# A long depthwise convolution accumulated in a PSUM bank, with GpSimd making the low parts of the weights

## The chip, the cores and the metric

The kernel runs on one core of one Trainium2 chip. The metric is the time of one execution on the device in microseconds (us), lower is better. The core has five engines that each work through an instruction list of their own in order: TensorE (PE in the profile, PEld for its weight loads), VectorE (DVE), ScalarE (ACT), GpSimd (POOL) and the DMA queue of SyncE (SP). They wait for one another by semaphores. SBUF holds the operands; PSUM has 8 banks of 128 x 512 float32, into which TensorE writes its products.

## The reference, cut to what matters

512 tokens of width 1024 go through two transformer blocks in float32. The second block, where the change lies, is one long set of products of the same normalised input with a wide projection, in eight parts of 1024 features, and what is made of them:

```python
g    = (h @ W3 + b3) * sigmoid(h @ W4 + b4)   # gated input
c    = dwconv(g, b_conv)                      # causal, depthwise, 31 taps:
                                              # c[f, t] = conv_b[f] + sum_j w[f, j] * g[f, t - 30 + j]
c    = silu(group_norm(c) * ...)              # group = 128 features
v    = layer_norm(gelu(h @ Wv + bv))          # mixed over the tokens by ws
u    = gelu(h @ W0 + b0)
za   = silu(h @ W2 + b2) * u * (mix(v) + ...)
m1   = sigmoid(h @ W6 + b6) * (za @ w_pa)     # and so on: z_b, m2, output projection
```

## The kernel before

**Layout.** Activations are feature-major: a tile `a` is 128 features by 512 tokens, and 1024 features are eight tiles, counted by `m`. A weight comes in pieces of 128 x 1024 (tile `wr`) by DMA. Each float32 product is done as three passes in a rounded format: every operand is split into a high and a low part. For a weight piece ScalarE casts the high part (`wh<-wr`, a CAST) and a second engine subtracts it to get the low part (`wl<-wr,wh`, a TENSOR_TENSOR). So a piece costs TensorE 8 k-tiles x 3 passes = 24 matmuls, and it can't go through the second operand of any k-tile before its `wl` is there. There are three buffers each for `wr`, `wh` and `wl`.

**Who makes the low part.** `weight` counts the pieces; of every four, `SHARE[0]` go to GpSimd and the others to VectorE, from the start of the second block until the products `m1` are done, `SHARE[1]` after that. It is (3, 0) before: three of four on GpSimd in the stage.

**The stage.** `block2` runs these phases on TensorE, one after the other: the gated input (8 steps of two pieces each), v (two halves of the features, 4 pieces each), u (8 pieces), za (8 pieces, each with four small matmuls for the token mix), m1 (8 steps of two pieces each). VectorE evacuates what each step leaves in PSUM, and at the end of each step it gets some taps of the convolution from `taps(n)`: one tap is one `scalar_tensor_tensor` on 128 x up to 512 elements, accumulator = gated input * weight + accumulator, 31 of them one after the other for each `m`, the first a `tensor_scalar` that adds the bias. `TAPS` says how many taps each phase's steps get. What of a convolution is finished goes through `group_norm`: split (a ScalarE cast waits for the last tap), two matmuls against a centring matrix, a square, a sum, a reciprocal root (`pow` on GpSimd, the tiles `s`).

**The order.** The kernel's code is traced once, and a scheduler in the framework puts the instructions of each engine in a fixed order by its own model of costs; taps of two convolutions may so alternate on VectorE. At run time no engine reorders anything. All instructions are recorded in one helper, so that the profile gives line L95 for nearly everything; the tiles' names tell them apart. In the stage `wl` is the low part of a weight piece, `a<-a,vecs,a` on VectorE a tap, and `a<-ps,vecs,a` 128x512 an evacuation from PSUM.

Of the kernel before, what the change touches and what calls it, by code (L numbers as in the profile page):

```python
# [27 lines left out]
# columns of the per-feature vectors, one array [128, NV]  # L28
# [9 lines left out]
_FIRST = 8  # columns that the first product needs  # L38

TAPS = (4, 3, 6, 6, 11)  # taps of the long convolution per step of each phase of the second block  # L40
# units of the attention after which the other projections follow
FILL = (0, 2, 8, 10, 4, 6, 12, 14, 14, 15, 17, 20, 23, 26, 30)
BANKS = {"score": (0, 1, 2, 3), "turn": (4, 5), "out": (6,), None: (7,)}  # PSUM banks by use
A_AT = (0, 2)  # steps of the values' projection after which a unit of the attention starts
SHARE = (3, 0)  # of four weight pieces, how many GpSimd splits: during the convolution, after it
RAW = 2  # m-tiles of the second block that are scaled after the product
# [7 lines left out]
class _Slot:  # L54
    """A slot of a pool, returned to it when its last view is dropped."""
# [8 lines left out]
class V:  # L64
    """A view of a tile that keeps its slot."""
# [38 lines left out]
class _Slots:  # L104
    """Slots of one pool, given out in program order, the one longest free first."""
# [15 lines left out]
class Body:  # L121
    """Activations are kept feature-major: features on partitions, the 512 tokens on the free axis.

    A float32 product is carried by three float32r passes: each operand is split exactly into a
    high and a low part, and high*high + high*low + low*high is accumulated in PSUM.
    """
# [36 lines left out]
    def weight(self, src, raw=None):  # L163
        """One [128, <=1024] piece of a weight: loaded and split."""
        nc = self.nc
        n = src.shape[-1]
        raw = raw or self.load(src)
        hi = self.whi.tile([P, 1024], F32R)
        lo = self.wlo.tile([P, 1024], F32R)
        nc.scalar.copy(hi[:, :n], raw[:, :n])  # L170
        self.pieces += 1
        eng = nc.gpsimd if self.pieces % 4 < self.share else nc.vector
        eng.tensor_tensor(lo[:, :n], raw[:, :n], hi[:, :n].bitcast(F32), op=ALU.subtract)
        return hi, lo

    def split(self, x, gain=None, out=None):
        """x (times a per-partition gain) in two exact parts."""
        nc = self.nc
        shape = list(x.shape)
        hi, lo = out if out else (self.a(shape, F32R), self.a(shape, F32R))  # L180
        if gain is None:
            nc.scalar.copy(hi, x)
            nc.vector.tensor_sub(lo, x, hi.bitcast(F32))
        else:
            nc.scalar.activation(hi, x, AF.Identity, bias=0.0, scale=gain)
            nc.vector.scalar_tensor_tensor(lo, x, gain, hi.bitcast(F32), op0=ALU.mult, op1=ALU.subtract)
        return hi, lo

    def mm(self, ps, l, r, start, stop):
        """l, r: pairs (hi, lo) of APs."""  # L190
        nc = self.nc
        nc.tensor.matmul(ps, l[0], r[0], start=start, stop=False)
        nc.tensor.matmul(ps, l[0], r[1], start=False, stop=False)
        nc.tensor.matmul(ps, l[1], r[0], start=False, stop=stop)

    def dense(self, src, rhs, n=S, raw=None):
        """One m-tile of W^T x: src = list of (weight piece, its k-tiles)."""
        ps = self.ps((P, n))
        k, last = 0, len(rhs) - 1
        for piece in src:  # L200
            w = self.weight(piece, raw)
            raw = None
            for kk in range(piece.shape[-1] // P):
                s = slice(kk * P, (kk + 1) * P)
                self.mm(ps, (w[0][:, s], w[1][:, s]), rhs[k], k == 0, k == last)
                k += 1
        return ps

    def square_sum(self, x, acc, last=False, scale=1.0):
        """Adds the squares of x to the list acc: one running sum and the last square apart."""  # L210
        nc = self.nc
        sq = self.a(x.shape)
        nc.scalar.activation(sq, x, AF.Square, scale=scale)
        if last or not acc:
            acc.append(sq)
        else:
            nc.gpsimd.tensor_tensor(acc[0], acc[0], sq, op=ALU.add)

    def token_sum(self, acc, n):
        """Sums over the partitions, token-major: [128, n]."""  # L220
        ps = self.ps((P, n))
        for j, t in enumerate(acc):
            for i in range(n):
                self.nc.tensor.matmul(ps[:, i:i + 1], t[:, i * P:(i + 1) * P], self.ones[:, 0:1],
                                      start=(i == 0 and j == 0), stop=(i == n - 1 and j == len(acc) - 1))
        acc.clear()
        return ps
# [9 lines left out]
    def bcast(self, r, n):  # L237
        """A token-major column per token tile, over all partitions: PSUM [128, n*128]."""
        ps = self.ps((P, n * P))
        for i in range(n):  # L240
            self.nc.tensor.transpose(ps[:, i * P:(i + 1) * P], r[:, i:i + 1].to_broadcast([P, P]), self.ident)
        return ps
# [46 lines left out]
    def nsa(self):  # L289
# [13 lines left out]
        # the first product goes on as x comes in  # L303
# [11 lines left out]
        def shifted(p):  # L315
            """Two m-tiles of a compression input: [(token parity, 64), token] of each group."""
# [13 lines left out]
        def token_gates():  # L330
            """Rows 0:48 from the weights' high parts, 64:112 from the low ones; turned and added."""
# [14 lines left out]
        def hidden(key, c2, between):  # L346
            """gelu(blocks W1), transposed: PSUM [hidden half, 2, (group, block)]."""
# [41 lines left out]
        def cmp_values(c2, between):  # L389
            """Per group [(head, block), head, (high, low)], zero outside of a head's own rows."""  # L390
# [25 lines left out]
        def values(q):  # L416
            """Values of the two dense branches, token-major: [t, group, (high, low)]."""
# [56 lines left out]
        def compressed_a(g):  # L474
            """Compressed branch of one group: probabilities, [t, t tile, head, block]."""
# [25 lines left out]
        def compressed_b(s):  # L501
            """Transposed and split: [(head, block), t]."""
# [5 lines left out]
        def dense_a(h, b):  # L508
            """Exponentials of one dense branch of one head, t tile by t tile, and their sums."""
# [4 lines left out]
            for tiles in ((0, 1), (2,), (3,)):  # L514
# [6 lines left out]
                # the blocks on the diagonal; those of the first two tiles lie side by side  # L521
# [18 lines left out]
        def dense_b(es):  # L540
            """Transposed and split: (parts, first column, columns, first token) per key tile."""
# [20 lines left out]
        # probabilities of the last two key tiles, of two units in turn; their first block stays zero  # L562
# [8 lines left out]
        def dense_c(h, b, parts, pc):  # L571
            """Product with the values; all three branches of a head in one bank."""
# [24 lines left out]
        # projections of the compression's inputs, statistics of x meanwhile  # L597
# [127 lines left out]
    def residual(self, src, rhs, x, gain, scale=None):  # L725
        """x + rhs W, m-tile by m-tile; its split parts times the gain; its squares' sum."""
# [95 lines left out]
    def conv(self, acc, src, taps, first, last, width, eng):  # L822
        """Taps first..last-1 of a causal depthwise convolution; tap width-1 is the current token."""
# [35 lines left out]
    def block2(self, x3, xs, acc, acc2, gain):  # L859
# [32 lines left out]
        hc, cacc, yb = [], [], []  # L892
# [3 lines left out]
        def taps(n):  # L896
            """The next taps of the convolution."""
            nonlocal done
            end = min(len(work), done + n)
            while done < end and work[done][0] < len(hc):  # L900
                m, j = work[done]
                w = self.vec("b_conv", 31 * m + 30 - j)
                if j == 0:
                    cacc[m] = self.a()
                    nc.vector.tensor_scalar(cacc[m], hc[m], w, self.vec("conv_b", m), op0=ALU.mult, op1=ALU.add)
                else:
                    acc = cacc[m][:, j:S]
                    nc.vector.scalar_tensor_tensor(acc, hc[m][:, 0:S - j], w, acc, op0=ALU.mult, op1=ALU.add)
                done += 1
                if j == 30:  # L910
                    hc[m] = None

        def group_norm(m):
            """Normalised over the group's channels and times the gain; in steps."""
# [27 lines left out]
        # gated input of the convolution  # L942
        self.share = SHARE[0]
        for m in range(KD):
# [20 lines left out]
            taps(TAPS[0])  # L965
        # v, token-major: gelu, layer norm, spatial mix
# [36 lines left out]
        # the layer norm's shift passes the mix as shift * (sum of a row of ws); bs added  # L1003
# [87 lines left out]
        # per-layer embedding  # L1091
# [18 lines left out]
        # the last projection by halves of the tokens: one half is normalised and stored under the other  # L1110
# [83 lines left out]
def _mt(w):  # L1194
    """[K, N] -> [N/128, 128 (k), K/128 * 128 (n)]"""
# [4 lines left out]
def _tok(w):  # L1200
    """[K, N] -> [N/512, K/256, 128 (k), 2 * 512 (n)]"""
# [73 lines left out]
```

## Time and profile before

| | |
|---|---|
| timed runs | 1505.55, 1504.51, 1504.46 us; median 1504.51 us |
| profiled execution | span 1505.2 us (no other time is listed for it) |
| PE busy | 1437.1 us, 95% |
| DVE busy | 977.6 us, 65% |
| ACT busy | 654.7 us, 43% |
| POOL busy | 403.4 us, 27% |
| instructions | 18564 |

TensorE is busy in 95% of the span, so a kernel of the same products can at best lose what TensorE idles, and what it spends at a lower clock. The page's strips of 40 slices show both in one place: PE falls from 9 tenths to 7 or 8 in the slices from 900 to 1240 us, which is the stage above, and DVE reads 9 there for four slices in a row, which it does nowhere else. The views of the next section but one are taken from there.

### The profile page before, as it was taken

The page shows a single profiled execution, that of the slowest core. Times are in us where ns is not written, and L with a number is a line of the kernel's source. Part 1 is how long each engine was busy: PE and PEld are TensorE (multiplying, and loading weights), DVE is VectorE, ACT ScalarE, POOL GpSimd, SP SyncE. Part 2 cuts the span into 40 slices and gives each one's busy share as a digit, 9 for nine tenths or more (in the row PEclk, how much of TensorE's full clock was granted, in tenths as well). Part 3 has the DMA queues.
Part 4 walks back from the last instruction along what each step waited for, and adds up shares of the span by engine and source line. Part 5 has one row for each costly group of instructions (what it writes and reads, how often), then busy time and mean ns, then how long its engine had stood idle before and what let it go on. Part 6 is the DMA issues. An engine that isn't in the chain of part 4 may idle for free. (4 is left out here: it accounts for less than half of the span.)

```text
span 1505.2 us, 18564 instructions
## 1 busy us (share of the span) xinstructions
PE 1437.1 (95%) x7106; PEld 1197.1 (80%) x7106; DVE 977.6 (65%) x1431; ACT 654.7 (43%) x1127; POOL 403.4 (27%) x333
## 2 busy tenths in 40 slices
PE   7999999999999999999999998897998899999997
PEld 6787778888888888888888887675886778888897
DVE  4868898885455465555533359999769953444564
ACT  4857778774344333323233333112233354432362
POOL 4022446451211311111111242333343441011213
PEclk9999999999999999999999999998999999999998
DMA  5241112114222333333333342221321222333331
GB/s 201 84 126 57 43 30 70 57 57 151 79 76 87 98 97 94 95 96 97 95 101 91 108 123 70 83 72 56 98 82 59 76 79 84 112 98 99 98 98 57
DMA packets 41385, 133.00 MB, mean 88 GB/s; under 512 B 5200, under 2 KB 7504, under 8 KB 41296
## 3 DMA queue, kind: packets, MB, share of 16 engines
q1 hardware_dynamic: 39568, 129.71, 28.5%
q10 hardware_dynamic: 1728, 2.10, 0.4%
q8 instruction: 56, 0.92, 0.2%
q14 instruction: 33, 0.27, 0.1%
HBM read 129.70 MB, written 2.10 MB: 88 GB/s over the span
## 5 line engine op out<-in xcount | busy, mean ns | idle before, releaser
L95 PE MATMUL ps<-a,wh 128*128 128x512 f32 (+1 forms) x3136 | 966.0, 390 | 9.4 <-ACT a L95 4.2
L95 PEld LDWEIGHTS ps<-a,wh 128*128 128x128 f32 x3136 | 588.3, 190 | 128.5 <-ACT a L95 5.4
L95 PE MATMUL ps<-a,wl 128*128 128x512 f32 (+1 forms) x1560 | 608.7, 390 | 22.6 <-DVE wl L95 14.9
L95 ACT CAST wh<-wr 128x1024 fp32r<-128x1024 f32 (+1 forms) x225 | 234.5, 1044 | 534.2 <-PE ps L95 351.5
L95 PEld LDWEIGHTS ps<-a,wl 128*128 128x128 f32 x1560 | 296.4, 190 | 84.9 <-DVE wl L95 17.4
L95 DVE TENSOR_TENSOR a<-ps,a 128x512 f32<-128x512 f32 (+5 forms) x284 | 169.8, 614 | 264.4 <-PE ps L95 210.3
L95 DVE TENSOR_TENSOR wl<-wr,wh 128x1024 fp32r<-128x1024 f32 x183 | 238.1, 1302 | 129.4 <-ACT wh L95 128.0
L95 POOL TENSOR_TENSOR a<-a,a 128x512 f32<-128x512 f32 (+1 forms) x106 | 138.9, 1314 | 597.8 <-ACT a L95 482.3
L95 DVE SCALAR_TENSOR_TENSOR a<-a,vecs,a 128x511 f32<-128x511 f32 (+25 forms) x332 | 288.3, 906 | 8.7 <-ACT a L95 6.3
L95 PE MATMUL ps<-a,a 128*128 128x256 f32 (+4 forms) x1180 | 209.2, 322 | 8.3 <-ACT a L95 8.3
L95 PEld LDWEIGHTS ps<-a,a 128*128 128x128 f32 x1180 | 165.3, 192 | 20.7 <-ACT a L95 10.6
L95 POOL TENSOR_TENSOR wl<-wr,wh 128x1024 fp32r<-128x1024 f32 x42 | 116.0, 2763 | 184.8 <-ACT wh L95 179.9
L95 POOL TENSOR_TENSOR a<-a,s 128x512 f32<-128x512 f32 (+3 forms) x140 | 115.3, 852 | 184.4 <-DVE s L95 106.6
L95 DVE TENSOR_TENSOR a<-a,a 128x512 fp32r<-128x512 f32 (+3 forms) x172 | 118.9, 697 | 23.7 <-ACT a L95 15.6
L95 ACT CAST a<-a 128x512 fp32r<-128x512 f32 (+1 forms) x124 | 76.4, 622 | 97.3 <-DVE a L95 78.6
L95 ACT ACTIVATE a<-a 128x512 f32<-128x512 f32 (+1 forms) x114 | 61.5, 551 | 117.9 <-DVE a L95 117.8
L95 PE MATMUL ps<-wh,a 128*128 128x512 f32 (+1 forms) x320 | 95.4, 379 | 6.7 <-ACT wh L95 6.7
L95 ACT ACTIVATE a<-ps,s 128x256 f32<-128x256 f32 (+4 forms) x148 | 77.5, 529 | 27.3 <-DVE s L95 23.7
L95 ACT CAST a<-ps 128x384 fp32r<-128x384 f32 (+2 forms) x132 | 62.9, 488 | 32.7 <-PE ps L95 27.5
L95 PEld LDWEIGHTS ps<-wh,a 128*128 128x128 f32 x320 | 59.8, 195 | 17.4 <-ACT wh L95 7.5
L95 DVE TENSOR_REDUCE s<-ps 128x1 f32<-128x128 f32 (+4 forms) x136 | 62.1, 491 | 5.1 <-PE ps L95 4.3
L95 PE MATMUL ps<-wl,a 128*128 128x512 f32 (+1 forms) x160 | 60.6, 379 | 4.3 <-DVE wl L95 2.7
(78 smaller groups left out, 611.6 us busy)
## 6 DMA issues: line engine op xcount, KB each, us to landing
wr<-in_w_in_dram SPq DMA_DIRECT2D x56, 512.0 KB, 3.6
wr<-in_ffn_gate_dram SPq DMA_DIRECT2D x22, 512.0 KB, 3.6
wr<-in_ffn_val_dram SPq DMA_DIRECT2D x22, 512.0 KB, 3.5
wr<-in_ffn_d_dram SPq DMA_DIRECT2D x16, 512.0 KB, 3.5
wr<-in_nsa_w_in_dram SPq DMA_DIRECT2D x15, 512.0 KB, 3.6
wr<-in_ca_wk_dram SPq DMA_DIRECT2D x8, 512.0 KB, 3.6
wr<-in_ca_wv_dram SPq DMA_DIRECT2D x8, 512.0 KB, 3.5
wr<-in_nsa_w_out_dram SPq DMA_DIRECT2D x8, 512.0 KB, 3.6
```

What stands on the lines that cost most here:

```text
L95: return lambda *a, **k: f(*[_raw(x) for x in a], **{n: _raw(x) for n, x in k.items()})
```

## The change

The accumulator of a convolution is a tile of PSUM instead of SBUF, and one copy by ScalarE (`to_sbuf`) brings it to SBUF after the last tap. GpSimd makes all low parts of the stage. The taps per step change from 4, 3, 6, 6, 11 (gated input, v, u, za, m1) to 4, 5, 5, 4, 10, with 7 in place of 4 from the third step of the gated input on. Comments are left out as well, which changes no instruction.

```diff
-TAPS = (4, 3, 6, 6, 11)  # taps of the long convolution per step of each phase of the second block
+TAPS = (4, 5, 5, 4, 10, 7)
...
-SHARE = (3, 0)  # of four weight pieces, how many GpSimd splits: during the convolution, after it
+SHARE = (4, 0)
...
-        hc, cacc, yb = [], [], []
+        hc, cacc, yb, run = [], [], [], [None]
...
                 if j == 0:
-                    cacc[m] = self.a()
-                    nc.vector.tensor_scalar(cacc[m], hc[m], w, self.vec("conv_b", m), op0=ALU.mult, op1=ALU.add)
+                    run[0] = self.ps()
+                    nc.vector.tensor_scalar(run[0], hc[m], w, self.vec("conv_b", m), op0=ALU.mult, op1=ALU.add)
                 else:
-                    acc = cacc[m][:, j:S]
+                    acc = run[0][:, j:S]
                     nc.vector.scalar_tensor_tensor(acc, hc[m][:, 0:S - j], w, acc, op0=ALU.mult, op1=ALU.add)
                 done += 1
                 if j == 30:
                     hc[m] = None
+                    cacc[m] = self.to_sbuf(run[0])
+                    run[0] = None
...
-            taps(TAPS[0])
+            taps(TAPS[0] if m < 2 else TAPS[5])
```

VectorE has 1400 instructions instead of 1414 and ScalarE 980 instead of 972. The first place is VectorE's list in the gated input, around the evacuation of the fourth to fifth step. In the kernel before, `a_8192` and `a_8688` are the accumulators of the first two convolutions (in SBUF), `a_8189` and `a_8262` their inputs, `wl_8514` is the low part of a weight piece, and `a_8472<-ps_8440` the evacuation:

```order
L95 SCALAR_TENSOR_TENSOR a_8192<-a_8189,vecs,a_8192 128x498
L95 TENSOR_TENSOR wl_8514<-wr_8511,wh_8513 128x1024
L95 SCALAR_TENSOR_TENSOR a_8192<-a_8189,vecs,a_8192 128x497
L95 SCALAR_TENSOR_TENSOR a_8688<-a_8262,vecs,a_8688 128x500
L95 SCALAR_TENSOR_TENSOR a_8192<-a_8189,vecs,a_8192 128x496
L95 SCALAR_TENSOR_TENSOR a_8688<-a_8262,vecs,a_8688 128x499
L95 SCALAR_TENSOR_TENSOR a_8192<-a_8189,vecs,a_8192 128x495
L95 SCALAR_TENSOR_TENSOR a_8472<-ps_8440,vecs,a_8471 128x512
```

With the change the same place reads as follows; `ps_8192` and `ps_8558` are the accumulators, now in PSUM, and `a_8478<-ps_8446` is the evacuation of that step:

```order
L95 SCALAR_TENSOR_TENSOR ps_8192<-a_8189,vecs,ps_8192 128x498
L95 SCALAR_TENSOR_TENSOR ps_8558<-a_8262,vecs,ps_8558 128x500
L95 SCALAR_TENSOR_TENSOR ps_8192<-a_8189,vecs,ps_8192 128x497
L95 SCALAR_TENSOR_TENSOR ps_8558<-a_8262,vecs,ps_8558 128x499
L95 SCALAR_TENSOR_TENSOR ps_8192<-a_8189,vecs,ps_8192 128x496
L95 SCALAR_TENSOR_TENSOR a_8478<-ps_8446,vecs,a_8477 128x512
L95 SCALAR_TENSOR_TENSOR ps_8192<-a_8189,vecs,ps_8192 128x495
L95 SCALAR_TENSOR_TENSOR ps_8558<-a_8262,vecs,ps_8558 128x498
```

The weight's low part has left VectorE's list; the taps of two convolutions alternate as before, and 13 to 15 of them stand between two evacuations of this phase, against 13 to 17 and a `wl` in every second step before.

The second place is ScalarE's list at the start of the phase m1. Before, `a_9774` is the gate of the first step, `a_10357<-a_9842` the cast at the start of a group norm (it waits for a last tap, `a_9842` being that accumulator), and `wh_9898` the high part of the first piece of `w_pa`:

```order
L95 CAST wh_9866<-wr_9864 128x1024
L95 ACT_TABLE_LOAD
L95 ACTIVATE a_9774<-ps_9775,vecs 128x512
L95 CAST a_10357<-a_9842 128x512
L95 CAST wh_9898<-wr_9896 128x1024
```

With the change, `a_9795` is that gate, `a_10045<-ps_9741` the new copy of a finished accumulator, and `wh_9917` the first piece of `w_pa`:

```order
L95 CAST wh_9885<-wr_9883 128x1024
L95 ACT_TABLE_LOAD
L95 ACTIVATE a_9795<-ps_9796,vecs 128x512
L95 COPY a_10045<-ps_9741 128x512
L95 CAST wh_9917<-wr_9915 128x1024
```

The cast of a weight piece stands directly behind an instruction that waits for VectorE's last tap, as it did before; a second such place is new, at the start of za, where `a_9349<-ps_9113` stands ahead of the cast of the piece `wh_9396`.

The third place is GpSimd's list at the start of the gated input, where `s_8069` and `s_8081` are the two reciprocal roots of the normalisation that the stage starts with, and the `wl` are low parts; lines with a plus are new there, those with a minus are gone:

```order
 L95 TENSOR_TENSOR s_8069<-s_8067,neghalf 128x4
+L95 TENSOR_TENSOR wl_8232<-wr_8229,wh_8231 128x1024
 L95 TENSOR_TENSOR s_8081<-s_8079,neghalf 128x4
 L95 TENSOR_TENSOR wl_8273<-wr_8270,wh_8272 128x1024
 L95 TENSOR_TENSOR wl_8304<-wr_8301,wh_8303 128x1024
```

One low part that VectorE made has moved in between the two roots.

## Rows read from the trace of the kernel before

**Rows 1.** The page: the span, and the busy time of each engine with its share of the span and its number of instructions.

```profile
span 1505.2 us, 18564 instructions
PE 1437.1 (95%) x7106; PEld 1197.1 (80%) x7106; DVE 977.6 (65%) x1431; ACT 654.7 (43%) x1127; POOL 403.4 (27%) x333
```

**Rows 2.** The stage in windows (start:end, length; then for PE, PEld, DVE, ACT and POOL the busy us and the number of instructions; the granted TensorE clock, the busy share of the DMA engines, GB/s).

```profile
900.00:920.00 20.00, 15.20 (x58) 11.39 (x57) 19.31 (x27) 8.65 (x11) 3.57 (x2) 0.91 0.24 79
920.00:960.00 40.00, 40.00 (x178) 33.16 (x177) 40.00 (x42) 9.72 (x11) 16.33 (x6) 1.00 0.31 93
960.00:1060.00 100.00, 79.95 (x317) 63.01 (x316) 98.89 (x139) 20.02 (x24) 30.46 (x10) 0.90 0.20 63
1060.00:1120.00 60.00, 60.00 (x285) 50.36 (x284) 36.67 (x38) 20.72 (x26) 26.15 (x12) 1.00 0.33 95
1120.00:1180.00 60.00, 48.16 (x211) 38.27 (x210) 59.63 (x71) 19.23 (x26) 20.15 (x10) 0.94 0.20 63
1180.00:1240.00 60.00, 58.38 (x279) 48.00 (x278) 46.65 (x60) 30.71 (x37) 26.80 (x13) 1.00 0.27 80
```

**Rows 3.** The stretches of the stage in which TensorE was granted the lower of its two clock levels (0.50 or 0.51 of 2.4 GHz, that is 1.2 GHz), in windows with the same columns.

```profile
909.20:912.60 3.40, 3.04 (x7) 2.47 (x8) 3.40 (x7) 0.89 (x1) 0.00 (x0) 0.50 0.04 14
970.60:977.50 6.90, 3.14 (x8) 2.48 (x9) 6.76 (x12) 0.00 (x0) 0.00 (x0) 0.51 0.30 88
1018.40:1025.30 6.90, 4.44 (x10) 3.16 (x11) 6.90 (x6) 2.66 (x3) 5.11 (x2) 0.51 0.27 76
1052.50:1059.40 6.90, 5.61 (x13) 4.46 (x14) 6.83 (x12) 0.00 (x0) 1.23 (x1) 0.51 0.27 76
1137.90:1141.30 3.40, 2.99 (x7) 2.41 (x8) 3.32 (x6) 2.15 (x3) 0.77 (x1) 0.50 0.51 146
1172.00:1175.40 3.40, 3.40 (x9) 2.64 (x10) 3.40 (x6) 0.00 (x0) 0.00 (x0) 0.50 0.78 245
```

**Rows 4.** What TensorE waited for from 900 to 1240 us: engine, tile and line waited for, us in total, times, longest.

```profile
PE ps L95 <- DVE wl L95: 16.0, 5, 7.1
PE ps L95 <- POOL wl L95: 9.3, 5, 5.2
PE ps L95 <- ACT wh L95: 6.7, 3, 4.1
PE ps L95 <- ACT a L95: 4.2, 2, 3.3
PE ps L95 <- DVE a L95: 2.1, 3, 0.8
```

**Rows 5.** VectorE's costliest groups from 914 to 1224 us that the change touches (taps, low parts of weights, first taps), and GpSimd's low parts from 880 to 1240 us: line, engine, operation, out<-in, shape, number; busy us, mean ns of one; idle before and what ended it.

```profile
L95 DVE SCALAR_TENSOR_TENSOR a<-a,vecs,a 128x499 f32<-128x499 f32 (+22 forms) x240 | 213.9, 941 | 1.3
L95 DVE TENSOR_TENSOR wl<-wr,wh 128x1024 fp32r<-128x1024 f32 x11 | 15.3, 1392 | 0.5 <-ACT wh L95 0.5
L95 DVE TENSOR_SCALAR a<-a,vecs 128x512 f32<-128x512 f32 x8 | 8.4, 1058 | 0.0
...
L95 POOL TENSOR_TENSOR wl<-wr,wh 128x1024 fp32r<-128x1024 f32 x39 | 108.8, 2792 | 178.5 <-ACT wh L95 173.6 <-PE ps L95 4.9
```

**Rows 6.** VectorE beside GpSimd in the timeline (start, us, engine, operation, number), first around 963 us, then around 1481 us; in each the POOL row is what ran on GpSimd at the time.

```profile
962.63 0.72 DVE L95 SCALAR_TENSOR_TENSOR a<-a,vecs,a 128x491 f32<-128x491 f32 x1
963.27 0.74 DVE L95 SCALAR_TENSOR_TENSOR a<-ps,vecs,a 128x512 f32<-128x512 f32 x1
963.93 2.20 DVE L95 SCALAR_TENSOR_TENSOR a<-a,vecs,a 128x486 f32<-128x486 f32 x1
962.36 3.25 POOL L95 TENSOR_TENSOR wl<-wr,wh 128x1024 fp32r<-128x1024 f32 x1 [8.54 <-ACT wh L95]
...
1480.95 0.47 DVE L95 SCALAR_TENSOR_TENSOR a<-a,vecs,ps 128x256 f32<-128x256 f32 x1
1480.01 2.50 POOL L95 TENSOR_TENSOR a<-a,a 128x256 f32<-128x256 f32 x3 [0.85 <-ACT a L95]
```

**Rows 7.** The evacuations of two successive steps of the gated input on VectorE in the timeline; that at 963.27 us in the group above is the fourth of the same row of steps.

```profile
917.96 0.75 DVE L95 SCALAR_TENSOR_TENSOR a<-ps,vecs,a 128x512 f32<-128x512 f32 x1 [0.19 <-PE ps L95]
934.93 0.74 DVE L95 SCALAR_TENSOR_TENSOR a<-ps,vecs,a 128x512 f32<-128x512 f32 x1
```

**Rows 8.** Prices: a run of nine alternating taps and a run of four taps of one accumulator (timeline), one low part on GpSimd (timeline), an evacuation and a tap of nearly the same size, VectorE reading and writing PSUM, VectorE with its second input in PSUM on 256 elements, an instruction of VectorE on 128x4 elements, and ScalarE's copy of a PSUM bank (groups by shape: number, busy us, mean ns).

```profile
935.59 5.94 DVE L95 SCALAR_TENSOR_TENSOR a<-a,vecs,a 128x502 f32<-128x502 f32 x9
1065.60 3.05 DVE L95 SCALAR_TENSOR_TENSOR a<-a,vecs,a 128x497 f32<-128x497 f32 x4
1062.64 2.39 POOL L95 TENSOR_TENSOR wl<-wr,wh 128x1024 fp32r<-128x1024 f32 x1 [8.90 <-ACT wh L95]
L95 DVE SCALAR_TENSOR_TENSOR a<-ps,vecs,a 128x512 f32<-128x512 f32 x16 | 11.8, 744 | 14.8 <-PE ps L95 14.3 <-ACT a L95 0.5
L95 DVE SCALAR_TENSOR_TENSOR a<-a,vecs,a 128x510 f32<-128x510 f32 x8 | 5.9, 738 | 0.0
L95 DVE TENSOR_TENSOR ps<-ps,a 128x512 f32<-128x512 f32 x4 | 2.5, 683 | 0.0
L95 DVE SCALAR_TENSOR_TENSOR a<-a,vecs,ps 128x256 f32<-128x256 f32 x10 | 4.3, 474 | 2.2 <-ACT a L95 2.2
L95 DVE TENSOR_SCALAR s<-ps 128x4 f32<-128x4 f32 x3 | 0.4, 147 | 0.0
L95 ACT COPY a<-ps 128x512 f32<-128x512 f32 x2 | 1.1, 586 | 0.0
```

## The prediction, made before the result was known

> **What bounds the kernel now.** I read the page first: TensorE is busy for 1437.1 of 1505.2 us [rows 1], so all that a change outside of the products can save is its idle time and what it spends at the lower clock. The windows then say where that lies. From 900 to 1240 us TensorE idles 4.80 us (900 to 920), 20.05 us (960 to 1060), 11.84 us (1120 to 1180) and 1.62 us (1180 to 1240), 38.3 us together, and none from 920 to 960 and from 1060 to 1120 [rows 2]. [...] The same matmuls take half of that at the full clock, so the dips cost 22.62 / 2 = 11.3 us: 1.5 at the start, 6.6 from 960 to 1060, 3.2 after 1120. The stage has 38.3 + 11.3 = 49.6 us to give.
>
> What TensorE waits for is in the waits: 16.0 us for a low part that VectorE makes, 9.3 us for one that GpSimd makes, 6.7 us for a high part, 6.3 us for split activations [rows 4]. VectorE is the cause of more than the first. It is busy for 40.00 of 40, 98.89 of 100 and 59.63 of 60 us in the windows from 920 to 1060 and from 1120 to 1180 [rows 2], and it falls behind: its evacuations at 917.96 and 963.27 are three steps apart, 15.1 us for each [rows 6, 7], while TensorE needs 48 matmuls of 40.00 / 178 = 0.225 us, 10.8 us, for a step of two pieces [rows 2]. A low part in its list comes as late as VectorE is. The wait for a GpSimd piece is partly this too: the reciprocal root ahead of that piece in GpSimd's list waits for VectorE's statistics.
>
> And VectorE is so slow because it stands still. While GpSimd makes a low part (962.36, 3.25 us), an operation with one input in PSUM passes at its usual 0.74 us, while the tap after it, with two inputs in SBUF, takes 2.20 us instead of 0.72 [rows 6]. Near the end of the program the taps' other form, one input in SBUF and one in PSUM, takes 0.47 us while a GpSimd operation runs [rows 6], as in the mean of all ten of them, 474 ns [rows 8]. Over the stage the 240 taps after the first ones take 213.9 us, mean 941 ns [rows 5], against 735 ns or so for one left alone: four in a row take 3.05 us [rows 8]. That is 240 x 0.206 = 49 us of standing still or sharing.
>
> **The change part by part.**
>
> *Accumulator in PSUM.* A tap then has one SBUF input, the form that passed above. I take its own time as unchanged: 744 ns for an evacuation of 512 elements that reads PSUM, 738 ns for a tap of 510 from SBUF; a PSUM-to-PSUM operation takes 683 ns [rows 8]. The start-to-start distance is (5.94 - 0.73) / 8 = 0.65 us where two convolutions alternate and (3.05 - 0.73) / 3 = 0.77 us on one accumulator [rows 8]. That a chain through PSUM costs more no row shows. Below I put 0.77. Above I put 0.89: the 0.744 us of the PSUM reader and behind it the 0.147 us of a nearly empty instruction, as if the two did not overlap at all [rows 8]. I take 0.77 to 0.79, since the PSUM rows lie next to the SBUF ones. The gain of the part is 49 us of VectorE's time, not yet TensorE's.
>
> [...]
>
> *All low parts on GpSimd.* VectorE loses 11 of them from 914 to 1224 us, 15.3 us [rows 5], and three outside of that; more important, TensorE no longer waits for anything in VectorE's list except by a PSUM bank or an activation. GpSimd gets 14 x 2.39 = 33 us more [rows 5, 8], in a stage where it is busy for 3.57 + 16.33 + 30.46 + 26.15 + 20.15 + 26.80 = 123 us of 340 [rows 2]: about half. That a list of GpSimd pieces feeds TensorE is shown from 1060 to 1120 us: TensorE is busy for all 60.00 us [rows 2]. The piece between the two roots at the start delays the second by 2.4 us at most; it is hidden behind the first step's second product, by about 1 us, and would cost up to 1.4 us if that cover were missing.
>
> *New distribution.* In the gated input 13 to 15 taps lie between two evacuations (the order above): 16 operations at 0.65 us are 10.5 us against TensorE's 10.8. VectorE keeps pace where it took 15.1. In v 20 taps on one accumulator stand before the first half's evacuation: 15.4 us, against 4 x 24 x 0.225 = 21.6 us for the half's four pieces. Then the gap at 967 (7.1 us, the longest wait in rows 4), that at 1015 to 1022 and that of the reciprocal root lose their cause. I put 960 to 1060 at zero: 20.05 + 6.6 = 26.7 us saved.
>
> *Copies.* Eight of 0.586 us [rows 8] on an engine that is busy for a third of the stage [rows 2] cost nothing by themselves. But each waits for a last tap, and the casts of weights stand behind it. Two such places are near their limit: za's first piece and `w_pa`'s first piece. In za a step of VectorE is three evacuating operations of about 0.7 us and the 4 taps of 0.77, 5.2 us, plus up to 2 us for one of its two-SBUF operations that meets a low part, against 24 x 0.225 + 4 small matmuls, some 6.3 us for TensorE: a lag of up to 0.9 us a step, 4 to 7 us at the end of za. I count 1.5 us of waiting at the first place (0 to 4), 5 at the second (0 to 7), and the 3.2 us of clock that follow such a gap today. The 1.62 us from 1180 to 1240 stay. So 11.3 of 16.7 us are left after 1120; saved: 5.4 us.
>
> *PSUM.* One or two banks of eight are held by accumulators. v is where that is tight: its two halves take four each, and the fourth of the second half must wait for the first half's last evacuation. VectorE is at its place there with about a microsecond to spare; a miss costs 1 to 3 us.
>
> *Start.* The 4.80 and 1.5 us at 900 to 920 belong to the scaling and splitting of the activations, which nothing changes: kept.
>
> **Sum.** 49.6 us less 6.3 at the start and 11.3 after 1120 leave 32 us. 1505.2 - 32 = 1473.2 in the profiled execution's terms, whose span lies 0.7 us above the median of the timed runs (1504.5): **1472 us**.
>
> **The rivals.**
>
> *Partly given back (1486 to 1501 us).* The copies put ScalarE in VectorE's wake: where VectorE is 5 us late at each of four to six copies, TensorE waits as often, and each gap brings 3 us of lower clock, as 2.99 and 3.40 us of busy time at the lower clock behind the gaps after 1120 show [rows 3]. Four times 5 + 1.6 give back 26 us: 1498. For it: a cast that waits behind a group norm's split is the 6.7 us for high parts already [rows 4]. Against it: the first six copies have half a step or more of slack if VectorE keeps pace.
>
> *No gain (1501.5 to 1507.5).* If the taps still stood still beside GpSimd, the 14 more low parts would add blocks as fast as the 15.3 us leave. The 0.47 us beside a GpSimd operation speak against it [rows 6].
>
> *Slower.* One mechanism: a tap that reads and writes the same PSUM bank, 31 times in a chain, is slow. Before, VectorE spends (213.9 + 15.3 + 8.4) / 248 = 0.96 us for each tap [rows 5], and has 23.3 us idle from 1060 to 1120 to catch up in [rows 2]. So it decides from 0.96 + 23.3 / 248 = 1.05 us for each tap; at 1.15 us VectorE needs 25 us more than it has, and the time is about 1530. Against it stand the 683 ns of the operation within PSUM, which isn't chained, however [rows 8]. [...]
>
> *More than forecast (under 1460).* za keeps pace too, and only the start is left: 1504.5 - 43 = 1461; under that only if the start gained as well.
>
> **How the numbers follow.** I give the forecast, 1460 to 1486 us, 0.71; partly given back 0.14; no gain 0.04; slower 0.06; under 1460 us 0.05. The likeliest one's own range, from the bounds above: with both copies free 1504.5 - 43 = 1461; with a tap of 0.89, v and m1 lag by 3 us each, both copies cost their most (4 + 7 in place of 6.5) and one more dip of 3 us follows: 1472 + 6 + 4.5 + 3 = 1486. To hold 8 in 10 the range takes some of the partial case: 1460 to 1490. A measurement of this kernel tells about 0.2%, 3 us, from no change. Faster by more than that: 0.71 + 0.14 + 0.05 = 0.90; within it 0.04; slower 0.06.
>
> **What would show it.** Right: taps as `ps<-a,vecs,ps` with a mean of 0.70 to 0.75 us and none of 2 to 3 us; GpSimd's low parts at about 2.4 us, none of 4 to 8; no `wl` on VectorE before 1220 us; VectorE's evacuations in the gated input 10.8 us apart; TensorE idle for 10 to 14 us from 900 to 1240, its waits on `ACT wh` and the split activations, none on a VectorE `wl`; the lower clock near 909 and once or twice in the last third. Wrong: taps over 0.9 us (slower rival), long taps beside GpSimd (no gain), or a list of `ACT wh` waits behind the copies (partly given back).

## The result and the profile after

The changed kernel takes 1465.08 us (median of four runs, 1464.92 to 1465.96) against 1505.03 us for the kernel before, run beside it. The ratio is 0.9738 with a 95% interval of 0.9727 to 0.9750: 40 us faster, where 1472 us were forecast. The page of after, its span and busy times:

```profile
span 1463.2 us, 18587 instructions
PE 1424.6 (97%) x7106; PEld 1190.2 (81%) x7106; DVE 922.6 (63%) x1417; ACT 659.7 (45%) x1135; POOL 415.9 (28%) x347
```

The span is 42.0 us shorter than that of [rows 1], where the timed runs differ by 40. The windows of the stage, columns as in [rows 2], say where:

```profile
900.00:920.00 20.00, 15.19 (x58) 11.41 (x57) 18.64 (x27) 8.65 (x11) 6.18 (x3) 0.91 0.25 79
920.00:960.00 40.00, 40.00 (x178) 33.14 (x177) 37.15 (x58) 10.30 (x12) 17.82 (x8) 1.00 0.31 93
960.00:1060.00 100.00, 100.00 (x439) 82.09 (x438) 91.48 (x135) 30.09 (x37) 39.78 (x18) 1.00 0.31 90
1060.00:1120.00 60.00, 59.32 (x294) 49.84 (x293) 35.33 (x46) 22.76 (x32) 34.31 (x18) 1.00 0.28 82
1120.00:1180.00 60.00, 56.73 (x268) 46.08 (x267) 43.50 (x66) 30.39 (x38) 26.36 (x13) 1.00 0.29 86
1180.00:1240.00 60.00, 60.00 (x291) 49.99 (x290) 34.83 (x50) 32.93 (x40) 16.32 (x10) 1.00 0.30 85
```

From 960 to 1060 us TensorE is busy for all 100.00 us; it was 79.95. In the stage it idles 4.81 + 0.68 + 3.27 = 8.8 us in place of 38.3, so 29.5 us of idle time went. The granted clock is 1.00 in every window but the first, whose dip is the one of before. TensorE's busy total fell by 12.5 us (1437.1 to 1424.6) for the same 7106 matmuls. Most of that is the lower clock's: of the 11.3 us that the prediction counts for it in [rows 3], all but the 1.5 us at the start, 9.8 us, are gone. The other 2.7 us no view here assigns. 29.5 + 12.5 = 42.0, and TensorE's busy and idle time before and behind the stage is the same in both traces. What TensorE still waits for from 900 to 1240 us:

```profile
PE ps L95 <- ACT a L95: 4.1, 2, 3.3
PE ps L95 <- POOL wl L95: 2.4, 2, 1.8
PE ps L95 <- DVE a L95: 1.8, 3, 0.8
PE ps L95 <- ACT wh L95: 0.4, 1, 0.4
```

The 16.0 us for low parts of VectorE in [rows 4] are gone, those for GpSimd's went from 9.3 to 2.4. The groups that answer to [rows 5], VectorE from 914 to 1224 us and GpSimd's low parts from 880 to 1240 us:

```profile
L95 DVE SCALAR_TENSOR_TENSOR ps<-a,vecs,ps 128x483 f32<-128x483 f32 (+24 forms) x240 | 170.3, 735 | 4.5
L95 DVE TENSOR_SCALAR ps<-a,vecs 128x512 f32<-128x512 f32 x8 | 6.3, 804 | 12.7 <-ACT a L95 12.7
...
L95 POOL TENSOR_TENSOR wl<-wr,wh 128x1024 fp32r<-128x1024 f32 x53 | 126.9, 2395 | 170.3 <-ACT wh L95 161.5 <-PE ps L95 6.2 <-DVE a L95 2.6
```

The taps fell from 941 to 735 ns, and GpSimd's low parts from 2792 to 2395 ns, so a tap and a low part no longer stand still for each other. VectorE's evacuations of the gated input in the timeline:

```profile
928.62 0.75 DVE L95 SCALAR_TENSOR_TENSOR a<-ps,vecs,a 128x512 f32<-128x512 f32 x1 [1.31 <-PE ps L95]
939.50 0.75 DVE L95 SCALAR_TENSOR_TENSOR a<-ps,vecs,a 128x512 f32<-128x512 f32 x1 [0.43 <-PE ps L95]
950.38 0.75 DVE L95 SCALAR_TENSOR_TENSOR a<-ps,vecs,a 128x512 f32<-128x512 f32 x1 [0.55 <-PE ps L95]
```

They are 10.9 us apart, the pace of TensorE's steps, and each waits for TensorE; in [rows 6, 7] three steps took 15 us each. The engine that is late has changed sides.

### The profile page after: what moved, and what is told of

Same layout as the page of the kernel before. It is cut to its first block, busy times and chain, and to the rows that moved or that the text cites. A ratio compares the mean times of both kernels' runs of the same rounds, so it can differ in the third digit from the quotient of the medians.

```text
span 1463.2 us, 18587 instructions
## 1 busy us (share of the span) xinstructions
PE 1424.6 (97%) x7106; PEld 1190.2 (81%) x7106; DVE 922.6 (63%) x1417; ACT 659.7 (45%) x1135; POOL 415.9 (28%) x347
## 4 chain that ended last, share of the span: by engine, by line
PE 87%; DVE 7%; ACT 2%; issue 1%; POOL 1%; DMA 1%; POOLq 0%; SPq 0%; ACTq 0%
PE ps L95 87%; DVE a L95 5%; ACT a L95 1%; POOL a L95 1%; DVE wl L95 1%; DVE ps L95 1%; ACT wh L95 1%; DMA a<-in_x_dram 1%; POOL wl L95 0%; DMA a<-in_mem_dram 0%; POOL s L95 0%; DVE s L95 0%; POOLq L1272 0%; SPq L95 0%; DVE wh L95 0%
## 5 line engine op out<-in xcount | busy, mean ns | idle before, releaser
L95 DVE TENSOR_TENSOR wl<-wr,wh 128x1024 fp32r<-128x1024 f32 x169 | 219.2, 1298 | 124.5 <-ACT wh L95 123.1
L95 POOL TENSOR_TENSOR wl<-wr,wh 128x1024 fp32r<-128x1024 f32 x56 | 134.1, 2395 | 176.6 <-ACT wh L95 167.8
L95 DVE SCALAR_TENSOR_TENSOR ps<-a,vecs,ps 128x483 f32<-128x483 f32 (+24 forms) x240 | 170.3, 735 | 4.5
L95 DVE SCALAR_TENSOR_TENSOR a<-a,vecs,a 128x511 f32<-128x511 f32 (+3 forms) x92 | 73.3, 801 | 7.1 <-ACT a L95 6.2
```

The source lines that it names most:

```text
L95: return lambda *a, **k: f(*[_raw(x) for x in a], **{n: _raw(x) for n, x in k.items()})
```

## The experiments

The change has three parts that can be made one by one: the accumulator in PSUM, the share of GpSimd, the distribution of the taps. Together with the kernels before and after, the first six runs are all eight combinations. Each was run beside the kernel before on the same chip; the table gives the median and the ratio to it.

| accumulator in PSUM | all low parts on GpSimd | new taps | us | ratio (95%) |
|---|---|---|---|---|
| - | - | - | 1505 | 1 |
| yes | - | - | 1464.64 | 0.9734 (0.9719 to 0.9749) |
| - | yes | - | 1522.33 | 1.0112 (1.0095 to 1.0130) |
| - | - | yes | 1522.21 | 1.0115 (1.0081 to 1.0149) |
| - | yes | yes | 1539.68 | 1.0225 (1.0207 to 1.0244) |
| yes | yes | - | 1459.97 | 0.9697 (0.9679 to 0.9714) |
| yes | - | yes | 1461.14 | 0.9705 (0.9685 to 0.9725) |
| yes | yes | yes | 1465.08 | 0.9738 (0.9727 to 0.9750) |

**The accumulator alone.** Edit, to the kernel before:

```diff
-                    cacc[m] = self.a()
-                    nc.vector.tensor_scalar(cacc[m], hc[m], ...
+                    run[0] = self.ps()
+                    nc.vector.tensor_scalar(run[0], hc[m], ...
...
+                    cacc[m] = self.to_sbuf(run[0])
```

> The kernel before with one part of the change: the accumulator in a PSUM bank and the copy by ScalarE. GpSimd makes three of four low parts and the taps per step stay 4, 3, 6, 6, 11. Theory A (the taps stand still beside GpSimd because both inputs are in SBUF, and this is most of what the change removes): taps at 0.73 us instead of 0.94, VectorE has 49 us more, TensorE's gaps from 960 to 1060 us go; 1466 to 1478 us, with a few waits on VectorE's low parts left. Rival B (what counts is that TensorE no longer waits for a low part in VectorE's list): the low parts stay in that list, so 1490 to 1503 us. Rival C (the distribution of the taps is the cause): 1495 to 1505 us.

1464.64 us, all of the change's gain: 1.4 us under theory A's range of 1466 to 1478, and far from B's and C's. VectorE's taps and low parts from 914 to 1224 us, and TensorE's first wait:

```profile
L95 DVE SCALAR_TENSOR_TENSOR ps<-a,vecs,ps 128x511 f32<-128x511 f32 (+18 forms) x240 | 174.7, 737 | 5.6
L95 DVE TENSOR_TENSOR wl<-wr,wh 128x1024 fp32r<-128x1024 f32 x15 | 19.8, 1321 | 2.5 <-ACT wh L95 2.5
...
PE ps L95 <- DVE wl L95: 4.0, 1, 4.0
```

Low parts are still in VectorE's list, 15 of them, but TensorE waits for one only. So it was not that they stand in that list; it was that the list ran late.

**The share alone.** Edit:

```diff
-SHARE = (3, 0)
+SHARE = (4, 0)
```

> The kernel before with one part of the change: GpSimd makes all low parts of the stage. Accumulator in SBUF, taps per step as before. Theory A: each low part moved takes 1.39 us from VectorE and puts a block of about 2.15 us on its taps, so VectorE is 10 us busier, and TensorE's waits for low parts become waits for high parts and evacuations behind VectorE: 1498 to 1515 us, no gain. Rival B: 1470 to 1485 us. Rival C: 1500 to 1505 us.

1522.33 us: slower by 17 us, 7 us over theory A's range of 1498 to 1515, and far from rival B's. The taps, and the waits of TensorE:

```profile
L95 DVE SCALAR_TENSOR_TENSOR a<-a,vecs,a 128x511 f32<-128x511 f32 (+28 forms) x234 | 221.9, 1001 | 1.2
...
PE ps L95 <- POOL wl L95: 14.7, 7, 5.2
PE ps L95 <- ACT wh L95: 14.4, 4, 11.4
PE ps L95 <- DVE a L95: 10.4, 5, 6.6
```

With no low part left on VectorE its taps are longer still, 1.00 us, so that over the whole program it is as busy as before (977.0 against 977.6 us; theory A had 10 us more). TensorE waits 46 us in the stage (38.3 before), now for GpSimd's low parts, for high parts and for what VectorE writes. That VectorE's lateness is behind all three is my reading; the view names only what came last.

**The distribution alone.** Edit:

```diff
-TAPS = (4, 3, 6, 6, 11)
+TAPS = (4, 5, 5, 4, 10, 7)
...
-            taps(TAPS[0])
+            taps(TAPS[0] if m < 2 else TAPS[5])
```

> The kernel before with one part of the change: taps per step 4, 5, 5, 4, 10 and 7 from the third step of the gated input on. Accumulator in SBUF, three of four low parts on GpSimd. Theory A: VectorE is full from 920 to 1060 us either way, more taps in the gated input and in v make it later there and earlier in za: 1498 to 1512 us. Rival B: 1500 to 1505 us. Rival C: 1470 to 1485 us.

1522.21 us, 17 us slower, some 10 over theory A's range; the four runs spread more than others (1517.01 to 1527.74 us). More taps come in a phase in which VectorE had no room, and it has not caught up where it had before: from 1060 to 1120 us it was busy for 36.67 us and TensorE for all 60.00 [rows 2], and here

```profile
1060.00:1120.00 60.00, 53.73 (x238) 44.21 (x238) 59.44 (x67) 17.16 (x21) 24.94 (x9) 0.94 0.27 79
```

VectorE is busy for 59.44 us and TensorE idles 6.27 us, at a granted clock of 0.94.

**Share and distribution, accumulator in SBUF.**

> The changed kernel with its accumulator back in SBUF (no copy): GpSimd makes all low parts, the taps have the new distribution. Theory A: without the PSUM bank the rest of the change gains nothing: 1495 to 1515 us, taps with a mean of 0.95 us or more, a third of the waits back. Rivals B and C: most of the change's gain, 1466 to 1480 us.

1539.68 us. The two losses add (17 + 17), which is more than theory A's 1495 to 1515 allowed, and the contrary of B and C. TensorE's first wait here:

```profile
PE ps L95 <- POOL wl L95: 37.0, 10, 18.9
```

**Accumulator and share; accumulator and distribution.**

> Accumulator in PSUM and all low parts on GpSimd, taps per step as before (4, 3, 6, 6, 11). Theory A (the PSUM accumulator alone is the change; with it VectorE has room, so that neither the share nor the distribution moves the time): 1461 to 1468 us, VectorE 20 us less busy than with the accumulator alone, no wait for a low part of VectorE. Rival F (share and distribution only work together, each alone costs 17 us also with the PSUM accumulator): 1478 to 1485 us.

> Accumulator in PSUM and the new taps per step, three of four low parts on GpSimd. Theory A: 1461 to 1470 us, with one or two waits for a low part of VectorE, 0 to 6 us together. Rival F: 1478 to 1485 us.

1459.97 us, 1 us under theory A's range, and 1461.14 us, inside it; rival F falls. In the first VectorE is 12 us less busy than with the accumulator alone (924.8 against 936.6 us in the whole program), where theory A had 20. With the accumulator in PSUM, what costs 17 us without it costs nothing and perhaps gains 3 to 5 us. The two together gain nothing over the accumulator alone (0.9738 against 0.9734): the stall that after has near 1125 us (3.3 us) isn't in the run with accumulator and share and the old taps, in which TensorE is busy for 60.00 us from 1120 to 1180:

```profile
1120.00:1180.00 60.00, 60.00 (x288) 50.27 (x287) 52.98 (x76) 32.61 (x40) 27.90 (x14) 1.00 0.32 95
```

**No low part on GpSimd.** Edit, to the kernel before:

```diff
-SHARE = (3, 0)
+SHARE = (0, 0)
```

> The kernel before (accumulator in SBUF, old taps) with no low part of the stage on GpSimd: VectorE makes all of them. Theory A (taps are long only while GpSimd runs beside them): taps fall from a mean of 0.94 to 0.73 to 0.75 us although their operands still lie in SBUF; 39 low parts of 1.22 us (48 us) come onto VectorE and about 49 us of standing still go, so VectorE is as full as before and the time stays near it, 1490 to 1525 us. Rival D (taps on an accumulator in SBUF are slow by themselves, by their chain or by other traffic): the mean stays at 0.90 us or more and the time goes over 1535 us.

The taps give the answer. VectorE from 914 to 1224 us, accumulators in SBUF as before; then a window and TensorE's longest wait:

```profile
L95 DVE SCALAR_TENSOR_TENSOR a<-a,vecs,a 128x490 f32<-128x490 f32 (+26 forms) x237 | 164.4, 739 | 1.1
L95 DVE TENSOR_TENSOR wl<-wr,wh 128x1024 fp32r<-128x1024 f32 x52 | 64.5, 1240 | 9.3 <-ACT wh L95 9.3
...
960.00:1060.00 100.00, 100.00 (x441) 82.17 (x440) 98.64 (x152) 29.55 (x36) 1.42 (x1) 1.00 0.31 89
...
PE ps L95 <- DVE wl L95: 1.7, 1, 1.7
```

739 ns with both inputs in SBUF, against 941 in [rows 5]: a tap in SBUF isn't slow, it is slow beside GpSimd. Rival D falls. But the time was expected at 1490 to 1525 us and is 1453.65 (ratio 0.9656, 0.9639 to 0.9674), 51 us faster than before and 11 faster than the change, by one digit. TensorE idles 2.1 us in the stage, though VectorE is busy for 98.64 of 100 us. The expectation equated a full VectorE with a late one.

**Some on GpSimd.** Edit: SHARE (1, 0) and (2, 0), to the kernel before.

> The kernel before (accumulator in SBUF, old taps) with one of four low parts of the stage on GpSimd, between the run with none (1453.7 us) and before with three (1505). Theory L (each low part on GpSimd costs the time its share of the collisions, because VectorE is already full): a straight line, 17 us a quarter, about 1471 us. Theory T (VectorE has room for some collisions and only falls behind when it has none left): 1453 to 1460 us. Either way taps between 0.78 and 0.85 us in the mean.

> The same with two of four low parts on GpSimd. Theory L: about 1488 us. Theory T: 1458 to 1480 us, most of the rise between two and three.

1481.71 us (0.9847, 0.9827 to 0.9866) and 1491.79 us (0.9912, 0.9890 to 0.9934). Neither theory's shape is right. With 0, 1, 2, 3 and 4 of four low parts on GpSimd and the accumulator in SBUF the time is 1453.7, 1481.7, 1491.8, 1505 and 1522.3 us: a step of 28 us for the first quarter, then 10, 13 and 17. The stage in one window from 900 us to the same point of the program (the span's end less 265.2 us), for none, one and two of four:

```profile
900.00:1186.40 286.40, 284.32 (x1306) 235.20 (x1305) 275.87 (x400) 107.77 (x131) 25.29 (x14) 1.00 0.31 90
900.00:1214.90 314.90, 293.73 (x1305) 240.17 (x1305) 282.61 (x389) 107.39 (x131) 70.05 (x26) 0.97 0.27 82
900.00:1223.90 323.90, 295.14 (x1309) 239.45 (x1308) 289.66 (x381) 108.89 (x134) 97.79 (x38) 0.97 0.27 80
```

TensorE idles 2.1, 21.2 and 28.8 us in them, and 38.3 with three of four [rows 2]. The windows don't hold the same work of VectorE, so what the share does to it is read from the whole program; with none on GpSimd the page has

```profile
PE 1420.0 (98%) x7106; PEld 1187.7 (82%) x7106; DVE 956.9 (66%) x1473; ACT 656.3 (45%) x1127; POOL 293.3 (20%) x291
```

VectorE's busy time is 956.9, 963.0, 968.2 and 977.6 us with none, one, two and three of four, although each quarter takes 14 low parts of 1.24 us from it; the last quarter changes it no more (977.0). Over 1473 - 1431 = 42 pieces that is (977.6 - 956.9) / 42 = 0.49 us more for each piece given away, so by an estimate from these totals a piece on GpSimd makes VectorE stand still for about 1.24 + 0.49 = 1.7 us here. The work that was moved off VectorE cost it more than doing it (977.6 against 956.9 us). Why the first quarter costs most of the time isn't settled. What the trace shows is that in that run TensorE waits again for low parts of VectorE, five times, and twice for one of GpSimd:

```profile
PE ps L95 <- DVE wl L95: 12.4, 5, 4.5
PE ps L95 <- POOL wl L95: 7.6, 2, 5.4
...
1038.81 10.26 POOL L95 TENSOR_TENSOR wl<-wr,wh 128x1024 fp32r<-128x1024 f32 x1 [10.10 <-ACT wh L95]
```

The last line is the low part behind the 5.4 us. GpSimd takes 10.26 us for it (2.39 alone, [rows 8]), while VectorE runs 15 taps in 9.77 us from 1035.97 us on, 0.65 us each, the pace of [rows 8]. So there it is GpSimd that is held.

For the rest I take it that the scheduler's order is made without the collisions and leaves no slack for them, but no run tried that.

**Accumulator in PSUM, no low part on GpSimd.**

> Accumulator in PSUM with the copies, taps per step as before, no low part of the stage on GpSimd. Theory A (the PSUM bank only takes the taps out of GpSimd's way, so without GpSimd's low parts it is worth nothing): 1452 to 1458 us, the taps at 0.735 to 0.74 as in SBUF; the eight copies add nothing. Rival (the PSUM accumulator is worth something by itself): under 1451 us, or the copies cost: over 1460 us.

1457.45 us (0.9684, 0.9660 to 0.9708), in theory A's range and not faster than the run with the accumulator in SBUF (0.9656). The taps take

```profile
L95 DVE SCALAR_TENSOR_TENSOR ps<-a,vecs,ps 128x500 f32<-128x500 f32 (+21 forms) x237 | 169.7, 735 | 3.0
```

735 ns. PSUM is worth 40 us beside GpSimd's low parts (1505 to 1464.64) and nothing without them (1453.65 to 1457.45): two remedies for one collision.

**The start of the stage.** Edit, to the changed kernel:

```diff
-            R["b"] = self.to_sbuf(self.bcast(r, NT))
-            r3b = self.to_sbuf(self.bcast(r3, NT))
+            rb = self.bcast(r, NT)
+            R["b"] = self.to_sbuf(rb)
+            r3b = self.bcast(r3, NT)
...
-                nc.vector.scalar_tensor_tensor(f, t, gain(k), R["b"], op0=ALU.mult, op1=ALU.mult)
+                nc.vector.scalar_tensor_tensor(f, t, gain(k), rb, op0=ALU.mult, op1=ALU.mult)
                 R["s"].append(self.split(f))
+            for k, t in enumerate(R["x"]):
                 nc.vector.scalar_tensor_tensor(t, t, self.vec("final_norm", k), r3b, ...
```

> The changed kernel with the same remedy applied to the start of the stage: the scaled activations read the broadcast reciprocal root from its PSUM bank instead of an SBUF copy (one SBUF input less), and the eight scalings of the residual, which nothing at that place waits for, come after the splits instead of between them. Theory A: the operations of 2.8 us near 889, 897 and 904 us go, the splits end 6 us earlier, and with them the idle 4.8 us of TensorE and the 1.5 us at the lower clock behind it: 1458 to 1461 us. Rival: the subtractions, which keep two SBUF inputs, stand still in their place: 1462 to 1466 us.

1458.25 us (0.9684, 0.9668 to 0.9701), 7 us under the change and inside the forecast. The first window and the scalings of the residual:

```profile
900.00:920.00 20.00, 20.00 (x90) 16.58 (x89) 20.00 (x32) 8.14 (x10) 9.70 (x4) 1.00 0.33 87
...
L95 DVE SCALAR_TENSOR_TENSOR a<-a,vecs,ps 128x512 f32<-128x512 f32 x8 | 5.4, 735 | 0.0
```

TensorE idles no more in this window (4.81 in after), its clock stays at 1.00, and no such scaling is held: five of them that lie from 900 us on take 1589 ns in the mean in after. Which of the two edits does it, the PSUM operand or the later place, was not told apart.

**No GpSimd, and the scalings later.** The last edit's second half alone, on the run without GpSimd's low parts.

> The kernel before with no low part of the stage on GpSimd and the eight scalings of the residual moved behind the splits at the start of the stage. What TensorE idles there in the run without GpSimd's low parts is 2.0 us at 900 to 920 us; 1450 to 1453 us if the deferral takes it away, 1453 to 1455 if VectorE is late elsewhere in its place.

1455.47 us (0.9671, 0.9652 to 0.9690), not to be told from 1453.65. A miss: from 900 to 920 us TensorE idles 2.3 us as it did (2.0), waiting 2.2 us for one low part of VectorE. No kernel here is shown to be faster than the one before with SHARE (0, 0).

## Why the prediction was right, and where it wasn't

*What bounds.* Right in place, a little short in size. Of the 49.6 us, the start is left (4.8 us and 1.5 of clock) and 4.0 us of idle time more, so 39.3 of them went. The count's 11.3 us are half of the 22.62 us that TensorE is busy in the six stretches of [rows 3]; these show a granted clock of 0.50 or 0.51 of full speed, and no view gives a frequency. The halving is an estimate: 22.62 us for 54 matmuls are 0.42 us each, against 0.225 us at a clock of 1.00 [rows 2, 3]. The 42.0 us hold 2.7 us besides that the count of the dips lacks, since TensorE's busy time fell by 12.5 us and not by 9.8.

*The sum.* In its own terms the sum missed by more than the timed runs show. It gave 1473.2 us for the profiled execution, whose span is 1463.2, 10.0 us less: 4.2 us of idle time and 3.2 us of clock that were to stay behind the copies and at the end, and the 2.7 us of busy time. For the step to timed runs it took the 0.7 us by which the span lay above the median before. But the profiled run of after is timed at 1465.02 us with a span of 1463.2, and in every run of the experiments the time is 1.7 to 2.1 us above the span. So the profiled execution before was most likely one of the slower ones, and that the forecast came within 7 us of the timed runs is in part luck.

*Accumulator in PSUM: the taps' time.* Right in cause and size. 735 ns were taken for a free tap and 735 measured; four taps on one accumulator take

```profile
1109.10 3.06 DVE L95 SCALAR_TENSOR_TENSOR ps<-a,vecs,ps 128x499 f32<-128x499 f32 x4
```

(3.06 - 0.73) / 3 = 0.78 us from start to start, where 0.77 to 0.79 was taken. The slower rival had no ground: the chain through PSUM costs what it costs in SBUF (0.78 against 0.77 us [rows 8]), and its deciding 1.05 us was never near. The run with SHARE (0, 0) shows the cause itself, in SBUF: 739 ns.

*All low parts on GpSimd.* The step that failed in its reason. It was put down as a gain, "more important, TensorE no longer waits for anything in VectorE's list". Without the accumulator in PSUM it loses 17 us, and with it the waits that it was to end are one of 4.0 us. There the move gains 5 us with the old taps (1464.64 to 1459.97) and loses 4 with the new ones (1461.14 to 1465.08). A low part in the list of an engine that keeps pace cost little here.

*New distribution.* Also overrated: the sum credited it with part of the 26.7 us of the stretch from 960 to 1060 us. The accumulator alone gives all 20.05 us of idle time there (TensorE is busy for 100.00 us in that run too); the distribution alone loses 17 us.

*Copies.* The term that was mis-sized. It said that 11.3 us stay after 1120 us: 1.5 and 5 us behind the two copies, 3.2 us of clock, 1.62 us at the end. From 1060 to 1240 us 3.95 us stayed, and the granted clock stays at 1.00. The two copies:

```profile
1057.93 0.59 ACT L95 COPY a<-ps 128x512 f32<-128x512 f32 x1 [6.47 <-DVE ps L95]
1130.21 0.59 ACT L95 COPY a<-ps 128x512 f32<-128x512 f32 x1 [2.26 <-DVE ps L95]
```

ScalarE waits 6.47 us for the first, and TensorE idles 0.68 us behind it, at the start of za. For the second it waits 2.26 us, which TensorE doesn't feel. The other 3.23 us lie ahead of the second copy, where m1 begins:

```profile
1122.00:1130.00 8.00, 4.77 (x18) 2.77 (x17) 7.73 (x12) 4.16 (x5) 2.36 (x1) 1.00 0.07 11
...
1115.99 2.74 DVE L95 TENSOR_TENSOR a<-a,a 128x512 fp32r<-128x512 f32 x1
1123.00 0.62 ACT L95 CAST a<-a 128x512 fp32r<-128x512 f32 x1 [6.76 <-DVE a L95]
1123.67 0.49 PE L95 MATMUL ps<-a,wh 128*128 128x512 f32 x1 [0.83 <-ACT a L95]
```

They are four gaps, the longest of 1.76 us for a low part. The first product with `w_pa` waits for the last split of za, whose cast has kept ScalarE waiting 6.76 us for VectorE; the next weight piece is cast behind that split and is late too. So the lag of VectorE in za, estimated at 4 to 7 us, is there, and a source of it is the one that was named: a subtraction with two SBUF inputs takes 2.74 us beside a low part, where others of its form take 0.69. But it reaches TensorE through za's split, and for less; the second copy stands ahead of the second piece of `w_pa`, not of the first as the list was read.

*PSUM.* Right: the tight place in v cost nothing, TensorE is busy for all 100.00 us from 960 to 1060.

*Start.* Right: 4.81 us and its dip are left, and the run on the start shows that they too were VectorE's standing still or its order.

*What was not asked.* The prediction weighed what the edit does to VectorE's list, never whether GpSimd should make low parts at all. The row for that was there: 49 us of standing still against 39 low parts on GpSimd [rows 5], which are 48 us of work at the 1.22 us that one takes on VectorE when nothing holds it (the mean of the three left there from 914 to 1224 us in after). It says that GpSimd's help was worth nothing; the runs say that it was worth less than nothing.

## What to carry to other kernels

Before moving work to GpSimd, look at what VectorE's operations with two SBUF inputs take beside it: compare their mean with one left alone (941 against 739 ns for a tap here), and count the difference against the work that was moved. If it doesn't pay, either bring it back or put one operand of the many operations into PSUM; the two didn't add here (1453.65 and 1464.64 us for either one, 1457.45 for both). And an engine at 99% isn't late by that (without GpSimd's low parts VectorE is busy for 98.64 us of 100, and TensorE for all 100.00): look at whether its evacuations wait for TensorE or TensorE for them.

## What the runs showed of the hardware

- An operation with two inputs in SBUF stood still beside GpSimd even when it was tiny: in after one on 128x4 elements (`s<-s,s`) that starts at 882.48 us, during a low part, takes 2.16 us, and the next of its form, at 885.97 us with nothing on GpSimd, 0.16 us.
- One SBUF input was not enough in every form here. The `tensor_scalar` of SBUF into SBUF on 128x512 elements (`a<-a,s,s`) takes 1303 ns in the mean in after and 542 ns in the run without GpSimd's low parts:

```profile
L95 DVE TENSOR_SCALAR a<-a,s,s 128x512 f32<-128x512 f32 x8 | 10.4, 1303 | 0.5 <-POOL s L95 0.5
...
L95 DVE TENSOR_SCALAR a<-a,s,s 128x512 f32<-128x512 f32 x8 | 4.0, 542 | 0.9 <-POOL s L95 0.9
```

- PSUM has one price on VectorE here: the first tap, a `tensor_scalar`, takes 804 ns into PSUM where it takes 538 ns into SBUF with no low part on GpSimd, 0.27 us eight times. A tap of 510 elements takes 749 ns into PSUM and 740 ns into SBUF, in the same two runs, after and the one with SHARE (0, 0).
